# Moving the weight sums and differences of seven-product matmuls from VectorE to GpSimd, and shifting a prefetch by one step

## The chip, the cores and the metric

The kernel runs on one core of a Trainium2 chip. The metric is the device time of one execution in microseconds; three executions of the kernel before gave 2406.97, 2407.13 and 2408.5 us, so the median is 2407.13 us and the runs lie within 0.06% of each other.

## The reference

The program is a small diffusion backbone in float32 with two layers, 512 latent tokens and 256 context tokens, width 1024. Layer 0 is SwiGLU, short gated convolution, SwiGLU; layer 1 is SwiGLU, grouped-query attention, SwiGLU. Each of the six sub-layers normalizes, scales and shifts its input by vectors that come from a conditioning vector ("modulation"), and its output is added through a third such vector, the gate.

```
def swiglu(h, w_in, w_out):
    gate, up = jnp.split(h @ w_in, 2, axis=-1)
    return (jax.nn.silu(gate) * up) @ w_out

m_lat = (silu_c @ ada_w[i] + ada_b[i]).reshape(b, N_SUBLAYERS, N_MOD, 1, d)
h = norm_modulate(x_lat, norm_g[i, 0], m_lat[:, 0, 0], m_lat[:, 0, 1])
x_lat = x_lat + MACARON_WEIGHT * m_lat[:, 0, 2] * swiglu(h, ffn_w_in[i, 0], ffn_w_out[i, 0])
```

The first matmul of the SwiGLUs (1024 to 2 x 2816) and of the convolution (1024 to 3 x 1024) carries most of the arithmetic. The modulation weights `ada_w` are 1024 x 9216 for each layer.

## The kernel before, in words

**Stages.** The stages are named f00, c01, f02 (layer 0), f10, attention and f12 (layer 1); f12 handles only the 512 latent tokens, the others all 768. Activations lie with the width on the partitions and the tokens along the free axis, weights are the stationary operand. Every float32 operand is split into a high part and a low rest (`split`, line 188: the high part by ScalarE, line 189, the rest by VectorE, line 190), and every product is three matmuls (`mm3`, lines 861 to 863: high x high, high x low, low x high).

**The seven products.** The input matmul of f00, c01, f02, f10 and f12 is done by a Strassen scheme. For each column chunk c, two weight columns blocks (a gate block g and an up block u, 1024 x 128 each) are cut into two halves along the contraction: quarters 0 and 1 of g, 2 and 3 of u, each 128 x 512 in SBUF. Seven products M1 to M7, each of four contraction steps of three matmuls over half the tokens (384, in f12 256), replace eight. M1, M2, M4 and M7 need quarters or quarter results as they stand; M5, M6 and M3 need sums or differences. These are made in place in the raw weight tile (`add_product`, lines 368 to 397): for M5, quarter 0 becomes 0 minus 2 (line 373) and quarter 2 becomes 2 plus 3 (line 382); for M6, quarter 2 becomes 3 minus 0 (line 373 again, called at 385); for M3, quarter 1 becomes 1 minus 2. So each chunk takes four such operations of 128 x 512, three by line 373 and one by line 382. There are 88 chunks. In the first chunks of each stage the products are plain ("direct"), without sums. `product_order` (line 89) gives the order on TensorE; in the steady state it is M1(c), M2(c), M7(c-1), M5(c), M6(c), M4(c-1), M3(c-1). After groups of four chunks the output matmul of the SwiGLU comes in between ("out").

**Weights on their way.** Raw weights come from HBM by DMAs that SyncE issues (line 230) into five buffers `raw` (two more in f12). The split results go into a store of eight buffers ("granules", tag `w`, line 256). `w_fill` (line 268) makes granules in the order in which TensorE will use them, as far ahead as the store has room; at the beginning of f12 only three ahead (`AHEAD`). One granule serves one product.

**Evictions.** ScalarE and VectorE also empty PSUM: M1, M5 and M6 are copied by ScalarE (lines 1135, 1140, 1143), M2, M7, M3 and M4 are added to those copies by VectorE (lines 1137, 1146, 1151, 1204), the output matmuls by line 929 on VectorE.

**Modulation in the background.** From f00 on, modulation vectors of the later sub-layers are computed on VectorE beside the products: `ada_step` (line 522) multiplies a 128 x 512 tile `aw` of modulation weights with the conditioning vector and sums along the row (line 530, an instruction and a short accumulator read for each of up to two conditioning vectors). `bg` spreads these steps evenly over the products and output matmuls of a stage. The tiles come by DMAs which GpSimd issues (`ada_next`, line 504, DMA at line 509); they rotate through 4 buffers in f00, 2 in c01 and 5 in f02 and f10. At the end of step n the kernel asks for tile n + depth, into the buffer which step n has just read.

**Order.** TensorE and SyncE run in the written order throughout; VectorE and ScalarE do so in the opening of each stage. Elsewhere, and on GpSimd always, a scheduler fixes each engine's order when the program is built, by the written order and its own costs. At run time each engine works through its queue in that order, and an instruction that waits for a semaphore holds up all behind it on its engine.

Of the kernel before, what the change touches and what calls it, by code (L numbers as in the profile page):

```python
# [14 lines left out]
ALU = mybir.AluOpType  # L15
# [114 lines left out]
def backbone(ctx: ExitStack, tc: tile.TileContext, a: dict, out: bass.AP):  # L130
    nc = tc.nc
    act, dve, pe = nc.scalar, nc.vector, nc.tensor
# [21 lines left out]
    def ptile(name, shape=(P, 512)):  # L154
        pool, tag = bank[name]
        return pool.tile(list(shape), F32, name=f"ps_{name}", tag=tag)
# [31 lines left out]
    def split(dsth, dstl, src, pinned=False):  # L188
        hi = act.activation(dsth, src, AF.Copy)  # L189
        lo = dve.tensor_tensor(out=dstl, in0=src, in1=dsth.bitcast(F32), op=ALU.subtract)  # L190
        if pinned:
            tc.keep_in_program_order(hi)
            tc.keep_in_program_order(lo)
# [44 lines left out]
    def raw_used(n):  # L238
        raw_tiles[n][1] -= 1
        if not raw_tiles[n][1]:  # L240
            raw_tiles.pop(n)
            if n in raw_extra["held"]:
                raw_extra["open"] -= 1
            elif n not in raw_homes:
                raw_state["open"] -= 1
# [122 lines left out]
    def add_product(g, u, m):  # L368
        def quad(q):
            return raw_tiles[g if q < 2 else u][0][:, 0, slice(4 * (q % 2), 4 * (q % 2) + 4)]  # L370

        def sub(o, x, y):
            dve.tensor_tensor(out=quad(o), in0=quad(x), in1=quad(y), op=ALU.subtract)  # L373

        def make(dh, dl):
            if m == "M1":
                split(dh, dl, quad(0))
            elif m == "M2":
                split(dh, dl, quad(1))
            elif m == "M5":  # L380
                sub(0, 0, 2)
                dve.tensor_tensor(out=quad(2), in0=quad(2), in1=quad(3), op=ALU.add)
                split(dh, dl, quad(2))
            elif m == "M6":
                sub(2, 3, 0)
                split(dh, dl, quad(2))
            elif m == "M7":
                split(dh, dl, quad(0))
            elif m == "M4":
                split(dh, dl, quad(3))  # L390
            else:
                sub(1, 1, 2)
                split(dh, dl, quad(1))
                raw_used(g)
                raw_used(u)

        stream.append((None, None, 4, make))
# [103 lines left out]
    ada_chunks, ada_loaded, ahead = [], {}, {}  # L501
    silu_row = {}

    def ada_next(n):

        if n < ahead["limit"]:
            t, kh, j = ada_chunks[n]
            w = ada_loaded[n] = ahead["pool"].tile([P, 512], F32, name=f"aw{t}_{kh}_{j}", tag="aw", bufs=ahead["depth"])
            nc.gpsimd.dma_start(w, a["ada_t"][t, kh, j])  # L509
# [12 lines left out]
    def ada_step(n, i, hm, nv):  # L522

        t, kh, j = ada_chunks[n]
        w = ada_loaded.pop(n)
        col = 4 * (hm % 2) + j
        for v in range(nv):
            total = mods[i][:, hm // 2, col, v : v + 1]
            junk = ptile("S")
            ins = dve.tensor_tensor_reduce(out=junk, in0=w, in1=silu_row[kh][:, v, :], scale=1.0, scalar=total if kh else ada_b[:, i, hm // 2, col : col + 1], op0=ALU.mult, op1=ALU.add, accum_out=total)  # L530
            tc.keep_in_program_order(ins)
        ada_next(n + ahead["depth"])
        if kh and j == 3:
            ada_done.add((i, hm))

    def ada_list():


        tasks = [(i, hm) for i in range(2) for hm in range(18) if i or hm > 5]
        at = 0  # L540
        for key, end in ADA_BY.items():
            steps = []
            for kh in range(2):
                steps += [lambda kh=kh: silu_load(kh)] + [rest] * 3
                for t in range(at, end):
                    i, hm = tasks[t]
                    for j in range(4):
                        steps.append(lambda n=len(ada_chunks), i=i, hm=hm: ada_step(n, i, hm, mod_groups(i, hm // 2)))
                        ada_chunks.append((t, kh, j))
            ada_tasks.extend((at, go) for go in steps)  # L550
            at = end
# [1149 lines left out]
    with tc.tile_pool(name="apool", bufs=1) as apool, tc.tile_pool(name="g0", bufs=1) as gp, tc.tile_pool(name="qp", bufs=1) as qp, psum(A=3, B=1, C=3, S=1):  # L1701
# [24 lines left out]
        with tc.tile_pool(name="boot", bufs=1) as bp, aw_pool():  # L1726
            in_order()
            op = opening(0, 0)
# [166 lines left out]
```

## Time and profile before

| what | value |
|---|---|
| median of three runs | 2407.13 us |
| span of the profiled execution | 2405.2 us |
| TensorE busy (matmuls) | 2383.8 us, 99% |
| VectorE busy | 2033.0 us, 85% |
| ScalarE busy | 1164.8 us, 48% |
| GpSimd busy | 135.2 us, 6% |
| sums and differences on VectorE | 352 instructions, 181.5 + 60.4 us |
| loads of modulation tiles issued by GpSimd | 240, 129.1 us |

The span runs from the first to the last instruction of the profiled execution; the runs' times lie about 2 us above it. A row of the groups gives line, engine, operation, output and inputs, shape and count, then busy time and mean ns, then the idle time of that engine just before such instructions and what ended it. A row of the waits gives the total in us, how often, and the longest. A row of the windows gives, for a stretch in us from the start, each engine's busy time with its number of instructions, then the granted TensorE clock, the DMA share and GB/s. In the timeline a row is start, duration, engine, line, operation.

### The profile page before, as it was taken

The numbers are of one execution on the slowest core, as the hardware profiler recorded it, in microseconds if no ns is written. First come the engines' busy times: TensorE is split into PE (matmuls) and PEld (weight loads), VectorE is DVE, ScalarE is ACT, GpSimd is POOL, SyncE is SP. The second block draws the span as 40 slices with busy tenths as digits, with TensorE's granted clock in tenths as the row PEclk, the third lists the DMA queues.
The fourth block names the chain that finished last, engine by engine and source line by source line (L and its number), as shares of the span: only waits on it lengthen the run. The fifth ranks groups of instructions, "written<-read, shape, count | busy, mean of one in ns | idle before, by whom it ended". The sixth has DMA issues, their size and how long they took to land.

```text
span 2405.2 us, 37639 instructions
## 1 busy us (share of the span) xinstructions
PE 2383.8 (99%) x14303; PEld 2258.6 (94%) x14303; DVE 2033.0 (85%) x4018; ACT 1164.8 (48%) x2198; POOL 135.2 (6%) x256
## 2 busy tenths in 40 slices
PE   8999999999999999999999999999999999999998
PEld 6999999999999999999999999999998889999998
DVE  6989989978988888888887988888778987987787
ACT  5634334355535653433435543343355776555555
POOL 0001111100000001000000001101100000000000
PEclk9999999999999999999999999999999999999999
DMA  9234444430334123323432144443441101133331
GB/s 334 87 112 137 130 126 129 131 115 27 106 106 132 33 69 115 127 93 119 126 100 73 49 124 126 146 136 122 141 131 45 53 10 58 67 110 102 106 106 62
DMA packets 93062, 253.71 MB, mean 105 GB/s; under 512 B 10320, under 2 KB 18640, under 8 KB 92880
## 3 DMA queue, kind: packets, MB, share of 16 engines
q1 hardware_dynamic: 71984, 183.65, 23.5%
q0 software_dynamic: 20352, 67.12, 9.4%
q8 instruction: 112, 1.84, 0.3%
q14 instruction: 70, 0.57, 0.1%
q10 hardware_dynamic: 544, 0.52, 0.1%
HBM read 249.16 MB, written 2.10 MB: 104 GB/s over the span
## 4 chain that ended last, share of the span: by engine, by line
PE 92%; DVE 3%; ACT 2%; DMA 1%; issue 1%; SPq 0%; DVEq 0%; ACTq 0%
PE ps_A L861 16%; PE ps_A L862 16%; PE ps_A L863 16%; PE ps_C L862 11%; PE ps_C L861 11%; PE ps_C L863 11%; PE ps_B L863 3%; PE ps_B L861 3%; PE ps_B L862 3%; PE ps_T L1542 1%; DMA ada<-in_ada_w 1%; ACT pr L1525 0%; DMA raw<-in_ffn_w_in 0%; DVE w L190 0%; PE ps_O L861 0%
## 5 line engine op out<-in xcount | busy, mean ns | idle before, releaser
L189 ACT ACTIVATE w<-raw 128x512 fp32r<-128x512 f32 (+1 forms) x862 | 522.4, 619 | 721.0 <-PE ps_A L863 229.7
L190 DVE TENSOR_TENSOR w<-raw,w 128x512 fp32r<-128x512 f32 (+1 forms) x862 | 574.3, 679 | 119.7 <-ACT w L189 105.8
L509 POOL DMA_DIRECT2D aw<-in_ada_t x240 | 129.1, 538 | 1374.8 <-DVE mods L530 973.9
L373 DVE TENSOR_TENSOR raw<-raw,raw 128x512 f32<-128x512 f32 x264 | 181.5, 689 | 9.0 <-DMA raw<-in_ffn_w_in 4.9
L862 PE MATMUL ps_C<-gl,w 128*128 128x512 f32 (+1 forms) x548 | 188.5, 344 | 0.0
L861 PE MATMUL ps_C<-gh,w 128*128 128x512 f32 (+1 forms) x548 | 188.4, 344 | 0.0
L863 PE MATMUL ps_C<-gh,w 128*128 128x512 f32 (+1 forms) x548 | 188.2, 343 | 0.0
L861 PE MATMUL ps_A<-gh,w 128*128 128x512 f32 (+1 forms) x540 | 185.8, 344 | 0.6 <-DVE x L929 0.6
L862 PE MATMUL ps_A<-gl,w 128*128 128x512 f32 (+1 forms) x540 | 185.7, 344 | 0.0
L863 PE MATMUL ps_A<-gh,w 128*128 128x512 f32 (+1 forms) x540 | 185.5, 344 | 0.0
L530 DVE CUSTOM_DVE_ANT_0 ps_S<-aw,silu_row,packed 128x512 f32<-128x512 f32 x208 | 156.9, 754 | 2.4 <-DMA aw<-in_ada_t 1.0
L530 DVE CUSTOM_DVE_ANT_0 ps_S<-aw,silu_row,mods 128x512 f32<-128x512 f32 x208 | 156.8, 754 | 1.0
L929 DVE SCALAR_TENSOR_TENSOR x<-ps_C,gat,x 128x512 f32<-128x512 f32 (+1 forms) x158 | 99.5, 631 | 43.1 <-PE ps_C L863 42.7
L861 PE MATMUL ps_A<-tB11h,w 128*128 128x384 f32 (+1 forms) x400 | 130.8, 327 | 0.2 <-ACT tB11h L785 0.2
L862 PE MATMUL ps_A<-tB11l,w 128*128 128x384 f32 (+1 forms) x400 | 130.3, 326 | 0.2 <-DVE tB11l L786 0.2
L863 PE MATMUL ps_A<-tB11h,w 128*128 128x384 f32 (+1 forms) x400 | 130.4, 326 | 0.0
L862 PE MATMUL ps_C<-tB22l,w 128*128 128x384 f32 (+2 forms) x376 | 121.8, 324 | 0.0
L863 PE MATMUL ps_C<-tB22h,w 128*128 128x384 f32 (+2 forms) x376 | 121.7, 324 | 0.0
L861 PE MATMUL ps_C<-tB22h,w 128*128 128x384 f32 (+2 forms) x376 | 121.5, 323 | 0.0
L929 DVE SCALAR_TENSOR_TENSOR x<-ps_A,gat,x 128x512 f32<-128x512 f32 (+1 forms) x162 | 101.8, 637 | 17.0 <-PE ps_A L863 16.7
L863 PEld LDWEIGHTS ps_C<-gh,w 128*128 128x128 f32 x548 | 103.9, 190 | 12.3
L861 PEld LDWEIGHTS ps_A<-gh,w 128*128 128x128 f32 x540 | 102.4, 190 | 14.0 <-issue 1.0
(486 smaller groups left out, 6946.0 us busy)
## 6 DMA issues: line engine op xcount, KB each, us to landing
raw<-in_ffn_w_in SPq DMA_DIRECT2D x170, 512.0 KB, 3.7
aw<-in_ada_t POOLq DMA_DIRECT2D x240, 256.0 KB, 3.0
raw<-in_ffn_w_out SPq DMA_DIRECT2D x80, 512.0 KB, 4.1
raw<-in_conv_w_in SPq DMA_DIRECT2D x24, 512.0 KB, 3.7
ada<-in_ada_w SPq DMA_DIRECT2D x28, 256.0 KB, 5.7
raw<-in_attn_w_qkv SPq DMA_DIRECT2D x12, 512.0 KB, 4.9
raw<-in_ada_w SPq DMA_DIRECT2D x8, 512.0 KB, 6.8
silu_row<-in_crow POOLq DMA_DIRECT2D x8, 512.0 KB, 4.2
```

The source lines that it names most:

```text
L189: hi = act.activation(dsth, src, AF.Copy)
L190: lo = dve.tensor_tensor(out=dstl, in0=src, in1=dsth.bitcast(F32), op=ALU.subtract)
L373: dve.tensor_tensor(out=quad(o), in0=quad(x), in1=quad(y), op=ALU.subtract)
L509: nc.gpsimd.dma_start(w, a["ada_t"][t, kh, j])
L530: ins = dve.tensor_tensor_reduce(out=junk, in0=w, in1=silu_row[kh][:, v, :], scale=1.0, scalar=total if kh else ada_b[:, i, hm // 2, col : ...
L861: pe.matmul(ps, wh, xh, start=first, stop=False, **kw)
L862: pe.matmul(ps, wh, xl, start=False, stop=False, **kw)
L863: pe.matmul(ps, wl, xh, start=False, stop=last, **kw)
L929: dve.scalar_tensor_tensor(out=x, in0=p[:, o - off : o - off + w], scalar=gat[:, m, v : v + 1], in1=x, op0=ALU.mult, op1=ALU.add)
L1542: pe.transpose(pt[:, c, :], pr[:, (c0 + c) * P : (c0 + c + 1) * P], ident)
```

## The change

`sub` and the sum for M5 are issued on GpSimd instead of VectorE, with the same operands. `ada_step` n no longer asks for tile n + depth but for tile n - 1 + depth, into the buffer that step n - 1 has read; the first step of each stage asks for nothing. The 240 loads remain, each one step later.

```diff
         def sub(o, x, y):
-            dve.tensor_tensor(out=quad(o), in0=quad(x), in1=quad(y), op=ALU.subtract)
+            nc.gpsimd.tensor_tensor(out=quad(o), in0=quad(x), in1=quad(y), op=ALU.subtract)
...
             elif m == "M5":
                 sub(0, 0, 2)
-                dve.tensor_tensor(out=quad(2), in0=quad(2), in1=quad(3), op=ALU.add)
+                nc.gpsimd.tensor_tensor(out=quad(2), in0=quad(2), in1=quad(3), op=ALU.add)
                 split(dh, dl, quad(2))
...
             tc.keep_in_program_order(ins)
-        ada_next(n + ahead["depth"])
+        if n > ahead["start"]:
+            ada_next(n - 1 + ahead["depth"])
```

## The prediction

> **What bounds the kernel now.** I read the page first, then TensorE's waits, then the stages in windows.
>
> ```profile
> span 2405.2 us, 37639 instructions
> PE 2383.8 (99%) x14303; PEld 2258.6 (94%) x14303; DVE 2033.0 (85%) x4018; ACT 1164.8 (48%) x2198; POOL 135.2 (6%) x256
> DVE  6989989978988888888887988888778987987787
> ```
>
> TensorE is idle for 2405.2 - 2383.8 = 21.4 us in all. VectorE is the next engine, with slices at 90% or more. A busy TensorE need not be one at its own pace, so the pace has to be shown. The windows show it:
>
> ```profile
> 120.00:480.00 360.00, 360.00 (x2068) 344.85 (x2067) 328.61 (x697) 138.78 (x254) 41.41 (x77) 1.00 0.42 128
> 600.00:780.00 180.00, 180.00 (x1032) 176.21 (x1032) 161.95 (x360) 84.52 (x161) 10.76 (x20) 1.00 0.37 115
> 900.00:1260.00 360.00, 360.00 (x2067) 344.85 (x2066) 301.69 (x599) 136.82 (x251) 30.65 (x57) 1.00 0.37 113
> 1380.00:1740.00 360.00, 360.00 (x2067) 344.85 (x2066) 302.88 (x599) 138.73 (x254) 45.17 (x84) 1.00 0.43 132
> 2040.00:2100.00 60.00, 57.74 (x426) 54.13 (x426) 57.54 (x112) 35.87 (x76) 0.00 (x0) 1.00 0.17 59
> 2100.00:2340.00 240.00, 240.00 (x1680) 224.99 (x1679) 194.73 (x350) 125.15 (x253) 0.00 (x0) 1.00 0.33 108
> ```
>
> Columns after the length: PE, PEld, DVE, ACT, POOL. The three long SwiGLU stretches (f00 at 120, f02 at 900, f10 at 1380) put 2068, 2067 and 2067 matmuls through in 360 us, though VectorE is 91%, 84% and 84% busy in them. So TensorE's pace there doesn't depend on how full VectorE is. That is the heart of the forecast: relief for VectorE has nothing to buy in these stretches. Of these rows only 2040 to 2100, the opening of f12, has TensorE idle (60 - 57.74 = 2.3 us), with VectorE 96% full.
>
> Why VectorE's lateness doesn't reach TensorE is seen from ScalarE's waits and the timeline:
>
> ```profile
> ACT w L189 <- PE ps_A L863: 229.7, 154, 9.0
> ACT w L189 <- PE ps_C L863: 213.9, 111, 11.9
> ACT w L189 <- PE ps_B L863: 56.7, 69, 1.2
> ```
> ```profile
> 700.43 0.34 PE L861 MATMUL ps_B<-tB21h,w 128*128 128x384 f32 x1
> ...
> 702.28 0.68 DVE L382 TENSOR_TENSOR raw<-raw 128x512 f32<-128x512 f32 x1
> ...
> 702.54 0.34 PE L861 MATMUL ps_A<-tT3h,w 128*128 128x384 f32 x1
> ...
> 702.88 0.55 DVE L1137 TENSOR_TENSOR g<-ps_B,g 128x384 f32<-128x384 f32 x1
> ```
>
> In 154 + 111 + 69 = 334 of 862 splits ScalarE stood waiting for TensorE to give a granule back, which means that the store was full. M2 began at 700.43 and the next product at 702.54: a product takes 2.11 us, and seven granules ahead are 14.8 us of cover.
>
> **The change, part by part.**
>
> *Removed from VectorE.*
>
> ```profile
> L373 DVE TENSOR_TENSOR raw<-raw,raw 128x512 f32<-128x512 f32 x264 | 181.5, 689 | 9.0 <-DMA raw<-in_ffn_w_in 4.9 <-DMA raw<-in_conv_w_in 0.2
> L382 DVE TENSOR_TENSOR raw<-raw 128x512 f32<-128x512 f32 x88 | 60.4, 687 | 0.7
> L190 DVE TENSOR_TENSOR w<-raw,w 128x512 fp32r<-128x512 f32 (+1 forms) x862 | 574.3, 679 | 119.7 <-ACT w L189 105.8
> L189 ACT ACTIVATE w<-raw 128x512 fp32r<-128x512 f32 (+1 forms) x862 | 522.4, 619 | 721.0 <-PE ps_A L863 229.7 <-PE ps_C L863 213.9 <-DVE raw L373 68.1
> ```
>
> There are 264 + 88 = 352 instructions. The timeline's line 382 began at 702.28 and the next instruction at 702.88, so one takes 0.60 us of VectorE's queue: 352 x 0.60 = 211 us. On TensorE's path it is worth nothing in the five long stretches (idle 0) and at most the 2.3 us in f12's opening, plus the one wait of 0.6 us for line 929 in the last row of TensorE's waits below: a best case of about 3 us.
>
> *Added to GpSimd.* The trace has no GpSimd operation with two inputs. The nearest rows:
>
> ```profile
> L1884 POOL MEMSET const-float32-1.0<- 128x1 f32 x1 | 0.1, 98 | 0.0
> masks.py:197 POOL MEMSET ident<- 128x128 f32 x1 | 0.2, 204 | 103.4 <-DVE tl L637 103.4
> masks.py:199 POOL TENSOR_SCALAR_AFFINE_SELECT identb<-identb 128x128 f32<-128x128 f32 x1 | 0.3, 292 | 0.1
> masks.py:199 POOL TENSOR_SCALAR_AFFINE_SELECT ident<-ident 128x128 f32<-128x128 f32 x1 | 0.8, 772 | 0.1
> ```
>
> A write alone costs (204 - 98) / 127 = 0.83 ns per element, one read and a write (292 - 98) / 127 = 1.53 ns. A second read at the same difference of 0.70 ns makes 2.23 ns, or 0.10 + 512 x 2.23 ns = 1.24 us. The bounds are 0.88 us (the second read free) and 1.66 us (it doubles the instruction less its start). I take 1.24, since the added read is nearest to the read already seen. That is 352 x 1.24 = 436 us of new GpSimd work, 18% of the span: GpSimd is not the bound.
>
> [...]
>
> *Latency of the sums.* For M5 two operations take 2.5 us instead of 1.3, for M6 one takes 0.6 us more. The quarters that M5 overwrites are free once M1 is split, three granules earlier, so 6.3 us are there for 2.5. M6's difference waits for M5's split: 0.62 + 0.68 + 1.24 = 2.5 us against one product's 2.1, 0.4 us late, covered by the 14.8. Behind a ScalarE split that waits stand ScalarE's evictions (lines 1135, 1140, 1143); the tightest, M6's, must be done before M7, two products or 4.2 us later. Price: 0. In f12's opening the store is only three ahead and the cover is gone. TensorE's waits there:
>
> ```profile
> PE ps_C L861 <- ACT w L189: 0.7, 1, 0.7
> PE ps_C L863 <- DVE w L190: 0.5, 1, 0.5
> PE ps_A L861 <- DVE x L929: 0.6, 1, 0.6
> ```
>
> The first two rows lie there: the first f12 product with a sum (M5, bank C) was waited for already. Its two operations add 1.2 us if exposed, less what VectorE's relief gives back: bounds -2.3 and +1.8 (M6's 0.6 too), I take +1.0 us.
>
> *What a busy GpSimd does to VectorE.* Two rows show that they get in each other's way:
>
> ```profile
> 1836.75 0.69 DVE L190 TENSOR_TENSOR w<-raw,w 128x512 fp32r<-128x512 f32 x1 [0.33 <-ACT w L189]
> ```
> ```profile
> 1836.82 0.77 POOL masks.py:199 TENSOR_SCALAR_AFFINE_SELECT ident<-ident 128x128 f32<-128x128 f32 x1
> ```
>
> The same select that took 0.29 us beside an idle VectorE took 0.77 us when VectorE had begun a two-input operation 0.07 us earlier, and ended 0.15 us after it. GpSimd waited; the opposite order isn't in the trace. So one GpSimd operation costs VectorE between 0 (GpSimd always yields) and 1.24 us (VectorE stands for all of it). I take half, 0.62: part of VectorE's work, like line 1137, reads one operand from PSUM, and with VectorE 84 to 91% full GpSimd will mostly be the one that waits. Then VectorE loses 0.62 for each 0.60 that it saves: its load stays as it was, and so does its cover. With f00 as the fullest stretch: 49 + 16 = 65 operations (rows below), 328.6 - 39.0 + 40.3 = 330 of 360 us. Price: 0.
>
> *Loads one step later.*
>
> ```profile
> L509 POOL DMA_DIRECT2D aw<-in_ada_t x240 | 129.1, 538 | 1374.8 <-DVE mods L530 973.9 <-DVE c L1146 178.4 <-DVE g L1137 49.2
> aw<-in_ada_t POOLq DMA_DIRECT2D x240, 256.0 KB, 3.0
> ```
>
> GpSimd now waits for VectorE's step before nearly each load. With sums behind it in the queue, such a wait would hold the sums; asked one step later, the buffer is mostly free already. SP's queue is not passed. The lead shrinks to depth - 1 steps: three or four steps in the SwiGLUs, one in c01, where a load must issue (0.54) and land (3.0) within one step.
>
> ```profile
> 600.00:780.00 180.00, 26.06 (x64) 1.00 0.37 115
> ```
>
> That is line 530 alone in c01: 64 records, four to a step, 16 steps in 180 us, 11 us apart on average. 3.5 us, or 6.0 behind two sums, fits. Price: 0.
>
> **Sum:** 2405.2 + 0 (long stretches) + 1.0 (f12's opening) = 2406.2 us of span; the median lies 2407.13 - 2405.2 = 1.9 us above the profiled span: 2408.1 us.
>
> **The rivals.**
>
> *Slower: the shared way into SBUF fills VectorE.* Line 373 by stage (VectorE's part), a third of it to be added for line 382:
>
> ```profile
> 120.00:480.00 360.00, 33.25 (x49) 1.00 0.42 128
> 600.00:780.00 180.00, 16.57 (x24) 1.00 0.37 115
> 900.00:1260.00 360.00, 31.02 (x45) 1.00 0.37 113
> 1380.00:1740.00 360.00, 33.10 (x48) 1.00 0.43 132
> 2100.00:2340.00 240.00, 33.04 (x48) 1.00 0.33 108
> ```
>
> So 65, 32, 60, 64 and 64 operations. If each stops VectorE for its full 1.24 us, f00 needs 328.6 - 39.0 + 80.6 = 370.2 of 360 us and c01 161.95 - 19.2 + 39.7 = 182.4 of 180; the others (340, 344, 236 of 240) just fit. TensorE then follows VectorE: +10.2 + 2.4 = 12.6, about 2420 us. It decides from (360 - 328.6 + 39.0) / 65 = 1.08 us of VectorE per operation. At 1.66 us the five stretches would run over by 37.5, 15.9, 5.3, 10.7 and 22.5, together 92 us: 2499. For it speaks that all these operands lie in SBUF and the 0.77 us row; against it that most collisions should fall on GpSimd. Chance 0.27.
>
> [...]
>
> *Slower: late through GpSimd's queue.* Sums stand behind a load that still waits, or c01's tiles come late. If each of c01's 16 steps stood 3.5 us for its tile, VectorE would be at 162 + 56 = 218 of 180 us: +38, 2445. The distance of 11 us speaks against it. Chance 0.08.
>
> *Faster by over 0.2%.* 0.2% is 4.8 us, about what a measurement of this kernel can tell from no change. The idle time in reach is the 3 us above; to get 2402 the f12 opening would have to lose all its waits and the start (where a few sums lie among the first 120 us) some too. Chance 0.07.
>
> **How the numbers follow.** My forecast, within 0.2%: 0.58. Faster 0.07; slower 0.27 + 0.08 = 0.35. Its own range is 2405 to 2411. The range for all reaches from 2402, nearly the whole gain in reach, to 2440, which takes in the exclusion up to about 1.4 us per operation and leaves out its worse end and most of the late loads.
>
> **What would show it.** Right: the five stretches again hold 2068, 1032, 2067, 2067 and 1680 matmuls with TensorE idle 0; lines 373 and 382 stand under POOL at 1.1 to 1.4 us; VectorE's busy time is 1.9 to 2.1 ms, with its two-input rows longer. Wrong: matmuls of lines 861 to 863 wait for line 190 or 189 in f00 (exclusion), or line 530 waits for `aw` in c01 (late loads), or GpSimd rows of 2 us and more.

## The result and the profile after

The changed kernel takes 2451.34 us (median of 4 runs, 2450.06 to 2452.7), the kernel before 2407.05 us beside it. The ratio is 1.0185, 95% interval 1.0173 to 1.0197: slower by about 44 us. The forecast was 2408.1 us, in a range that ended at 2440.

The page of the changed kernel:

```profile
span 2448.3 us, 37886 instructions
PE 2395.6 (98%) x14303; PEld 2264.0 (92%) x14303; DVE 1997.3 (82%) x3666; ACT 1156.2 (47%) x2198; POOL 639.5 (26%) x608
```

VectorE has 352 instructions fewer, and its busy time fell, from 2033.0 to 1997.3 us. GpSimd is busy for a quarter of the span. Nevertheless TensorE's idle time rose from 21.4 to 2448.3 - 2395.6 = 52.7 us. So a total of busy time doesn't tell what happened; the windows tell where. These are the stretches of the prediction, columns PE, PEld, VectorE, ScalarE, GpSimd:

```profile
120.00:480.00 360.00, 351.69 (x2006) 335.66 (x2005) 316.19 (x613) 130.74 (x243) 130.52 (x137) 1.00 0.41 125
600.00:780.00 180.00, 171.51 (x962) 165.03 (x961) 155.61 (x299) 75.35 (x147) 60.54 (x51) 0.99 0.30 92
900.00:1260.00 360.00, 360.00 (x2067) 344.82 (x2066) 296.14 (x536) 138.00 (x251) 116.40 (x114) 1.00 0.35 109
1380.00:1740.00 360.00, 359.45 (x2056) 345.20 (x2056) 292.79 (x527) 145.68 (x266) 134.85 (x142) 1.00 0.42 129
2040.00:2100.00 60.00, 59.33 (x471) 57.27 (x470) 50.96 (x107) 37.65 (x76) 1.58 (x1) 1.00 0.19 63
2100.00:2340.00 240.00, 229.85 (x1598) 214.35 (x1597) 179.21 (x283) 117.40 (x251) 88.18 (x65) 0.99 0.30 99
```

Count matmuls: f00 has 2006 where there were 2068, c01 962 where there were 1032, f12 1598 where there were 1680. At 360/2068 = 0.174 us a matmul (f12: 240/1680 = 0.143) that is 10.8, 12.2 and 11.7 us. f02 lost none. f10 has 2056, but it was busy for 359.45 us of its window, which by now holds other products than before, since everything there begins some 28 us later. The two stretches that lost nothing or little, f02 and f10, have nearly as many GpSimd operations as f00 (60 and 64 against 65). Matching each matmul of one trace with the same one of the other gives the same picture: +10.9 us in f00, +12.4 in c01, +13.5 in f12, at most 0.4 in f02 and f10, the rest in the pieces between. Of the 43.3 us in all, 35.6 come in 24 single jumps of over 0.3 us (in the time from the start of one matmul to the next; two more at 7 and 11 us wait for a DMA). TensorE kept its pace and then stood still for a moment, 24 times.

The jumps come at fixed places. By the clock of the kernel before, those in f00's stretch lie at 186.5, 278.5, 370.5 and 462.5 us, one for each group of four chunks, at the first product behind the output matmuls. In f12 four lie 61.5 us apart, at the same place of each group, where M4 begins.

What TensorE stood for, from its waits (total, times, longest):

```profile
PE ps_A L862 <- DVE x L930: 12.2, 7, 2.5
PE ps_A L862 <- DVE c L1147: 11.7, 7, 2.6
PE ps_B L864 <- DVE w L190: 4.0, 3, 1.6
PE ps_A L862 <- ACT g L1136: 2.9, 2, 1.7
```

Lines behind 532 are one higher than before. The longest waits are not for a weight granule (line 190) but for evictions: a product wants bank A, and VectorE hasn't emptied it yet (line 930 after an output matmul; line 1147 after M7, whose result must be read before M4 adds to it).

And these are the groups that pay. The operations moved to GpSimd, the splits, the loads, one eviction, and line 373 by itself (shortest/median/longest):

```profile
L190 DVE TENSOR_TENSOR w<-raw,w 128x512 fp32r<-128x512 f32 (+1 forms) x862 | 701.1, 827 | 224.8 <-ACT w L189 215.2 <-PE ps_B L864 0.3
L373 POOL TENSOR_TENSOR raw<-raw,raw 128x512 f32<-128x512 f32 x264 | 367.9, 1394 | 868.1 <-DVE w L190 720.5
L382 POOL TENSOR_TENSOR raw<-raw 128x512 f32<-128x512 f32 x88 | 136.2, 1548 | 6.8
L509 POOL DMA_DIRECT2D aw<-in_ada_t x240 | 131.0, 546 | 589.9 <-DVE mods L530 417.6
L930 DVE SCALAR_TENSOR_TENSOR x<-ps_C,gat,x 128x512 f32<-128x512 f32 (+1 forms) x158 | 98.8, 628 | 42.9 <-PE ps_C L864 42.8
```
```profile
L373 POOL TENSOR_TENSOR raw<-raw,raw x264: 1263/1297/1925, 75.0 to 2398.5; 128x512 f32<-128x512 f32 x132
```

The split (line 190), which reads two tiles in SBUF, went from 679 to 827 ns. Line 930, which reads one operand from PSUM, stayed at 628 (631 before). Next come line 530's multiplications, which also read two tiles in SBUF, with 813 ns instead of 754. Nothing else of the program's work became longer to this extent.

The trace also shows it one by one. 178 splits of 128x512 began while a sum ran on GpSimd, and 175 of them ended between 0.54 and 0.56 us after that sum did, whenever they had begun. The 66 instructions of line 930 that ran beside a sum took as long as the others (740 ns against 746 at 128x512, 474 against 477 at 128x256).

One of the jumps, in f12, from the timeline:

```profile
2138.30 0.41 DVE L1138 TENSOR_TENSOR g<-ps_B,g 128x256 f32<-128x256 f32 x1
2138.51 1.26 POOL L373 TENSOR_TENSOR raw<-raw,raw 128x512 f32<-128x512 f32 x1 [3.16 <-DVE w L190]
2138.63 1.69 DVE L190 TENSOR_TENSOR w<-raw,w 128x512 fp32r<-128x512 f32 x1
...
2139.85 1.59 POOL L382 TENSOR_TENSOR raw<-raw 128x512 f32<-128x512 f32 x1
2140.24 0.41 DVE L1147 TENSOR_TENSOR c<-ps_A,c 128x256 f32<-128x256 f32 x1
...
2140.71 0.58 PE L862 MATMUL ps_A<-tT4h,w 128*128 128x256 f32 x1 [2.25 <-DVE c L1147]
```

GpSimd began its difference at 2138.51. VectorE began a split 0.12 us later, stood until GpSimd had ended at 2139.77, did its work in 0.55 us and was done at 2140.32: 1.69 us instead of 0.68. Behind the split in VectorE's queue was the eviction of bank A, and M4 waited for it. TensorE had been idle for 2.25 us, some 1.0 of them by this stop (1.69 - 0.68); the rest is lateness that the queue already had. GpSimd's next operation, begun at 2139.85 while VectorE was still at work, took 1.59 us where 1.26 to 1.30 are the rule: here a split held up GpSimd, by some 0.3 us.

### The profile page after: what moved, and what is told of

Read it like the earlier page. It is cut to its first block, busy times and chain, and to the rows that moved or that the text cites. A ratio compares the mean times of both kernels' runs of the same rounds, so it can differ in the third digit from the quotient of the medians.

```text
span 2448.3 us, 37886 instructions
## 1 busy us (share of the span) xinstructions
PE 2395.6 (98%) x14303; PEld 2264.0 (92%) x14303; DVE 1997.3 (82%) x3666; ACT 1156.2 (47%) x2198; POOL 639.5 (26%) x608
## 4 chain that ended last, share of the span: by engine, by line
PE 70%; DVE 14%; issue 9%; ACT 3%; DMA 2%; POOL 1%; SPq 0%; DVEq 0%; ACTq 0%; POOLq 0%
PE ps_A L862 13%; PE ps_A L863 13%; PE ps_A L864 12%; PE ps_C L862 8%; PE ps_C L863 8%; PE ps_C L864 8%; DVE w L190 4%; DVE ps_S L530 4%; PE ps_B L864 2%; PE ps_B L862 2%; PE ps_B L863 2%; DVE x L930 1%; POOL raw L373 1%; DMA ada<-in_ada_w 1%; ACT w L189 1%
## 5 line engine op out<-in xcount | busy, mean ns | idle before, releaser
L190 DVE TENSOR_TENSOR w<-raw,w 128x512 fp32r<-128x512 f32 (+1 forms) x862 | 701.1, 827 | 224.8 <-ACT w L189 215.2
L373 POOL TENSOR_TENSOR raw<-raw,raw 128x512 f32<-128x512 f32 x264 | 367.9, 1394 | 868.1 <-DVE w L190 720.5
L530 DVE CUSTOM_DVE_ANT_0 ps_S<-aw,silu_row,packed 128x512 f32<-128x512 f32 x208 | 170.1, 818 | 3.4 <-DMA aw<-in_ada_t 1.2
L530 DVE CUSTOM_DVE_ANT_0 ps_S<-aw,silu_row,mods 128x512 f32<-128x512 f32 x208 | 167.9, 807 | 1.9
L382 POOL TENSOR_TENSOR raw<-raw 128x512 f32<-128x512 f32 x88 | 136.2, 1548 | 6.8
L862 PE MATMUL ps_A<-tT4h,w 128*128 128x384 f32 (+1 forms) x352 | 117.4, 333 | 11.7 <-DVE c L1147 11.7
L189 ACT ACTIVATE gh<-g 128x384 fp32r<-128x384 f32 (+1 forms) x158 | 78.7, 498 | 90.9 <-DVE g L1205 46.1
```

Source lines behind the costliest of these rows:

```text
L373: nc.gpsimd.tensor_tensor(out=quad(o), in0=quad(x), in1=quad(y), op=ALU.subtract)
L382: nc.gpsimd.tensor_tensor(out=quad(2), in0=quad(2), in1=quad(3), op=ALU.add)
L862: pe.matmul(ps, wh, xh, start=first, stop=False, **kw)
```

## The experiments

The theory: a GpSimd operation that reads SBUF and a VectorE instruction with two SBUF inputs exclude each other, VectorE's queue stops for the rest of the GpSimd operation, and the evictions behind the stopped instruction come late for TensorE. The rivals: the loads that come a step later; the sums that come later, since they take GpSimd longer and cross two engines; another order of VectorE's queue, since the scheduler plans with other costs.

**The two parts of the change apart.** `loads_only` keeps the sums on VectorE; `sums_only` keeps the loads as before.

```diff
 loads_only, against the changed kernel
-            nc.gpsimd.tensor_tensor(out=quad(o), in0=quad(x), in1=quad(y), op=ALU.subtract)
+            dve.tensor_tensor(out=quad(o), in0=quad(x), in1=quad(y), op=ALU.subtract)
...
-                nc.gpsimd.tensor_tensor(out=quad(2), in0=quad(2), in1=quad(3), op=ALU.add)
+                dve.tensor_tensor(out=quad(2), in0=quad(2), in1=quad(3), op=ALU.add)
 sums_only, against the changed kernel
-        if n > ahead["start"]:
-            ada_next(n - 1 + ahead["depth"])
+        ada_next(n + ahead["depth"])
```

Expected of `loads_only`: 

> Only the loads one step later; the sums stay on VectorE. If the sums cost the time: 2406 to 2409 us, no change. If the later loads cost it (tiles of c01 come late): 2420 us or more, with line 530 waiting for aw in c01.

Expected of `sums_only`: 

> The sums and differences go to GpSimd, the loads of modulation tiles stay as they were (asked for at the end of step n for tile n + depth). If the sums cost the time, by exclusion from SBUF, by lateness or by the order in which the scheduler then puts VectorE's queue: 2440 to 2460 us, near the changed kernel's 2451. If the loads one step later cost it: 2407 us. If the shift of the loads protects the sums from waiting behind a load on GpSimd: slower than 2451, by up to some 20 us.

Measured: `loads_only` 2406.78 us, ratio 1.0001 [0.9992, 1.001]; `sums_only` 2448.45 us, ratio 1.0176 [1.0161, 1.0191]. The loads cost nothing; the sums carry all of it, within the 3 us between `sums_only` and the changed kernel.

**Late sums without reads.** In `write_only` the sums are left out on all engines. In their place, in the same tiles and with the same waits, GpSimd writes a constant three times. VectorE and ScalarE run the same instructions as in `sums_only`. Their order was expected to be the same too, but by the traces it isn't: some 80 of VectorE's 3666 instructions and some 65 of ScalarE's 2198 stand elsewhere. At 122 us, for instance, an eviction (line 1204 of `sums_only`) comes ahead of two splits instead of behind them.

```diff
-            nc.gpsimd.tensor_tensor(out=quad(o), in0=quad(x), in1=quad(y), op=ALU.subtract)
+            for _ in range(3):
+                nc.gpsimd.memset(quad(o), 0.5)
...
-                nc.gpsimd.tensor_tensor(out=quad(2), in0=quad(2), in1=quad(3), op=ALU.add)
+                for _ in range(3):
+                    nc.gpsimd.memset(quad(2), 0.5)
```

Expected: 

> Leaves out the sums: GpSimd writes a constant into the same quarter three times instead, with the same waits for it, so that it is about as long busy (an estimated 3 x 0.53 = 1.6 us from the memset rows) but reads nothing from SBUF. The scheduler gives VectorE and ScalarE exactly the order of sums_only. Exclusion theory: VectorE's two-input instructions are back at 0.68 us and the time at 2405 to 2415 us. Lateness theory (splits and what stands behind them wait for GpSimd): 2440 to 2460 us as with real sums. Order theory: also 2440 to 2460 us.

Measured: 2403.47 us, ratio 0.9987 [0.9978, 0.9997]. Its groups and a row of its waits:

```profile
L374 POOL MEMSET raw<- 128x512 f32 x792 | 410.6, 526 | 310.7 <-DVE w L190 286.6
L190 DVE TENSOR_TENSOR w<-raw,w 128x512 fp32r<-128x512 f32 (+1 forms) x862 | 574.4, 679 | 285.8 <-ACT w L189 274.0
```
```profile
ACT w L189 <- POOL raw L374: 126.1, 83, 4.8
```

Three writes take 3 x 0.526 = 1.58 us, longer than a sum did. ScalarE waits 126.1 us for GpSimd, VectorE in turn 274.0 us for ScalarE, and TensorE loses nothing: the store covers late sums, as the prediction had it. The split is back at 679 ns. What is missing here is GpSimd's reading. The run is not the whole proof, for two reasons: its order differs, and ScalarE waits longer in the changed kernel (173.1 + 60.5 = 233.6 us). The next pair has neither weakness.

**Reads without late sums.** `no_sums` leaves the sums out on all engines. `lock_only` leaves them out too, but GpSimd makes 352 operations with two SBUF inputs at their places, whose results no split reads (the splits of M7 and M3 take another quarter for that). VectorE's and ScalarE's instructions are the same in both, and by the traces so is their order, except for four of VectorE's instructions in c01.

```diff
 no_sums, against the changed kernel
-            nc.gpsimd.tensor_tensor(out=quad(o), in0=quad(x), in1=quad(y), op=ALU.subtract)
+            pass
...
-                nc.gpsimd.tensor_tensor(out=quad(2), in0=quad(2), in1=quad(3), op=ALU.add)
 lock_only, against the changed kernel
-                sub(0, 0, 2)
-                nc.gpsimd.tensor_tensor(out=quad(2), in0=quad(2), in1=quad(3), op=ALU.add)
+                beside(0, quad(0), quad(2))
+                beside(0, quad(2), quad(3))
...
-                sub(2, 3, 0)
+                beside(0, quad(3), lows[-1].bitcast(F32))
...
-                sub(1, 1, 2)
-                split(dh, dl, quad(1))
+                beside(1, quad(1), quad(2))
+                split(dh, dl, quad(2))
```

Here `beside` is a subtraction on GpSimd with the given operands, and `lows[-1]` is the low granule of the split just made.

Expected of `no_sums`: 

> Leaves out the sums altogether, on all engines; the splits read the quarters as they were loaded. VectorE's order differs from the changed kernel's in few places. Exclusion and lateness theories: 2403 to 2408 us, which is also the most that taking the sums off VectorE could ever bring. Order theory (evictions planned behind other work): 2430 us or more.

Expected of `lock_only`: 

> Leaves out the sums as no_sums does, with the same order on VectorE and ScalarE; beside the splits GpSimd does two-input operations of the same size, place and number (352), whose result no split reads, so that nothing on the way of a weight waits for GpSimd. No_sums was 2402.15 us. If exclusion from SBUF alone makes the loss: 2430 to 2455 us, with line 190 near 0.82 us. If it takes exclusion together with splits that wait for GpSimd: 2402 to 2412 us though line 190 is slow.

Measured: `no_sums` 2402.15 us, ratio 0.9982 [0.9973, 0.9992]; `lock_only` 2444.81 us, ratio 1.0158 [1.0141, 1.0175]. The difference of 42.7 us is made by operations that no compute engine waits for. (SyncE's loads of raw weights do wait for them, 77 times, but the weights don't come late: ScalarE waits 13.4 us for feed-forward weights in `lock_only`, 16.8 in `no_sums`.) Matched with `no_sums`, `lock_only` loses 11.0 us in f00, 9.9 in c01, 11.1 in f12 and at most 0.1 in f02 and f10: the same stages as the changed kernel, with nearly the same amounts.

`no_sums` also speaks against another order of the queues as the cause. Between it and the changed kernel some 40 of VectorE's instructions and 16 of ScalarE's stand elsewhere, only 2 of them in f00 and 6 in f12, and `no_sums` loses nothing in either stage.

From the pages, the groups and the windows (f00) of `no_sums`:

```profile
PE 2382.1 (99%) x14303; PEld 2258.5 (94%) x14303; DVE 1839.2 (77%) x3666; ACT 1167.9 (49%) x2198; POOL 135.1 (6%) x256
```
```profile
L190 DVE TENSOR_TENSOR w<-raw,w 128x512 fp32r<-128x512 f32 (+1 forms) x862 | 577.4, 679 | 251.5 <-ACT w L189 233.8
```
```profile
120.00:480.00 360.00, 360.00 (x2068) 344.81 (x2067) 296.27 (x630) 137.45 (x252) 41.41 (x77) 1.00 0.42 128
```

and of `lock_only`, with its windows for f00 and f02 and TensorE's first two waits:

```profile
PE 2395.3 (98%) x14303; PEld 2263.7 (93%) x14303; DVE 2068.3 (85%) x3666; ACT 1163.4 (48%) x2198; POOL 668.5 (27%) x608
```
```profile
L190 DVE TENSOR_TENSOR w<-raw,w 128x512 fp32r<-128x512 f32 (+1 forms) x862 | 740.3, 872 | 132.3 <-ACT w L189 123.3
```
```profile
120.00:480.00 360.00, 352.32 (x2005) 335.63 (x2004) 328.16 (x612) 130.84 (x241) 131.56 (x137) 1.00 0.41 125
...
900.00:1260.00 360.00, 360.00 (x2067) 344.81 (x2066) 307.35 (x532) 136.19 (x250) 119.34 (x115) 1.00 0.35 107
```
```profile
PE ps_A L863 <- DVE c L1148: 11.0, 9, 3.9
PE ps_A L863 <- DVE x L931: 9.2, 8, 2.2
```

VectorE does the same work in both, so the difference of its busy times is time in which it stood: 2068.3 - 1839.2 = 229 us, 0.65 us for each of 352 operations. In the changed kernel it is 1997.3 - 1839.2 = 158 us, 0.45 us each. TensorE waits for the same two evictions. The f00 row against that of the kernel before is the most instructive pair: VectorE is busy for 328.16 us here and for 328.61 us before, and here TensorE loses 63 matmuls, before none. Equal load, unequal loss.

**One input instead of two.** `lock_one_input` is `lock_only` with each operation replaced by two copies, each of which reads one tile (the sums stay left out).

```diff
-            nc.gpsimd.tensor_tensor(out=quad(o), in0=x, in1=y, op=ALU.subtract)
+            for t in (x, y):
+                nc.gpsimd.tensor_copy(quad(o), t)
```

Expected: 

> As lock_only, but each two-input operation is replaced by two copies with one input each (sums left out). If any GpSimd operation that reads SBUF stops VectorE's two-input instructions: line 190 above 0.75 us and 2425 us or more. If GpSimd needs two inputs for that: line 190 at 0.68 us and 2402 to 2405 us.

Measured: 2416.05 us, ratio 1.0039 [1.0024, 1.0054].

```profile
L376 POOL COPY raw<-raw 128x512 f32<-128x512 f32 x616 | 521.0, 864 | 684.4 <-DVE w L190 636.7 <-DVE bias L1230 24.9 <-ACT w L189 3.2
L190 DVE TENSOR_TENSOR w<-raw,w 128x512 fp32r<-128x512 f32 (+1 forms) x862 | 637.4, 749 | 197.1 <-ACT w L189 182.9
```

(The other 88 of the 704 copies read a granule and stand in a row of their own.) One read is enough to stop VectorE (749 ns against 679), though 704 copies cost only 13.9 us over `no_sums`. That lies between the two times that were expected: the stops came, but only a third of `lock_only`'s loss. Why is not shown.

**How the loss goes with the number of operations.** Three kernels make fewer of the sums on GpSimd: `f02_f10_only` those of f02 and f10, 160; `m5_on_vector` those for M6 and M3, 176; `m5_sum_on_vector` the three differences, 264.

```diff
 f02_f10_only: sub and the sum for M5 take an engine eng
+                add_product(raw[c, 0], raw[c, 1], m, nc.gpsimd if key in ("f02", "f10") else dve)
 m5_on_vector
+            (dve if m == "M5" else nc.gpsimd).tensor_tensor(out=quad(o), in0=quad(x), in1=quad(y), op=ALU.subtract)
 m5_on_vector and m5_sum_on_vector
-                nc.gpsimd.tensor_tensor(out=quad(2), in0=quad(2), in1=quad(3), op=ALU.add)
+                dve.tensor_tensor(out=quad(2), in0=quad(2), in1=quad(3), op=ALU.add)
```

Expected of `f02_f10_only`: 

> Sums on GpSimd in f02 and f10 alone, on VectorE in f00, c01 and f12. In the changed kernel's trace the stretches of f02 and f10 lost 0.0 and 0.4 us and their openings 1.8 each, so if each stage stands for itself: 2406 to 2411 us. If the loss moves with the order or with the total: 2420 us or more.

Expected of `m5_on_vector`: 

> Only the single differences of M6 and M3 (176) go to GpSimd; M5's pair stays on VectorE. If the loss goes with the number of stops: about half of the 44 us, 2422 to 2432 us. If it comes from the two back-to-back operations of M5, which keep VectorE out for up to 2.7 us at once: 2405 to 2413 us.

Expected of `m5_sum_on_vector`: 

> All three differences on GpSimd (264 operations), only M5's sum (line 382) on VectorE, so that no two GpSimd operations follow each other directly. The changed kernel with 352 lost 44 us, m5_on_vector with 176 lost 7. If the back-to-back pair makes the loss: 2410 to 2420 us. If the loss goes with the number or the total of the stops: 2430 us or more.

Measured: 2410.74 us, ratio 1.0017 [1.0008, 1.0026]; 2413.39 us, ratio 1.0027 [1.0016, 1.0037]; 2438.07 us, ratio 1.0128 [1.0112, 1.0143]. In `f02_f10_only` the long stretches lose 0.4 us between them; the loss lies in the openings of the two stages. So the first came out as expected for stages that stand for themselves. The second lies just above the range that it was given if M5's pair makes the loss, and the third in the range for the number or the total of the stops; the two don't agree on one of these causes. (The pairs of M5 took 2.65 us or more in the changed kernel, but its longest split took 2.08: none was seen to be kept out for a whole pair.) The third isn't a clean test, since its VectorE makes the sum for M5 and waits for GpSimd's difference first:

```profile
DVE raw L382 <- POOL raw L373: 92.0, 59, 3.1
```

So I took the clean kernels, `lock_only` cut in two. `lock_pair` keeps only the two operations at M5, one right behind the other, `lock_single` only those at M6 and M3; 176 each, the sums left out as in `no_sums`.

```diff
 lock_pair, against lock_only
-                beside(0, quad(3), lows[-1].bitcast(F32))
...
-                beside(1, quad(1), quad(2))
 lock_single, against lock_only
-                beside(0, quad(0), quad(2))
-                beside(0, quad(2), quad(3))
```

Expected of `lock_pair`: 

> Left out: all sums and differences of weight quarters, as in no_sums. GpSimd makes 176 operations with two SBUF inputs that nothing reads, at the places of M5's two, one right behind the other; the 176 of M6 and M3 are not made. VectorE and ScalarE run the same instructions in the same order as in no_sums (2402.2 us) and lock_only (2444.8 us). If the loss goes with the number of stops, half of lock_only's 42.6 us: 2421 to 2426 us, as in lock_single. If it is the back to back pair that makes VectorE late, most of it: 2435 us or more. If the loss grows faster than the number, as the sums on GpSimd suggest (176 of them cost 7 us, 264 cost 31, 352 cost 44): under 2415 us.

Expected of `lock_single`: 

> Left out: all sums and differences of weight quarters, as in no_sums. GpSimd makes 176 operations with two SBUF inputs that nothing reads, at the places of M6's and M3's differences, each alone; the pair of M5 is not made. VectorE and ScalarE as in no_sums. If the loss goes with the number of stops: 2421 to 2426 us, the same as lock_pair. If the pair of M5 makes it: 2403 to 2412 us. If the loss grows faster than the number: under 2415 us here and in lock_pair too.

Measured: 2411.64 us, ratio 1.0019 [1.001, 1.0029], and 2408.21 us, ratio 1.0005 [0.9996, 1.0014]. The page and f00 of `lock_pair`, then of `lock_single`:

```profile
PE 2383.8 (99%) x14303; PEld 2258.2 (94%) x14303; DVE 1951.0 (81%) x3666; ACT 1165.5 (48%) x2198; POOL 402.5 (17%) x432
```
```profile
120.00:480.00 360.00, 357.67 (x2052) 342.12 (x2051) 316.70 (x628) 135.48 (x248) 89.26 (x107) 1.00 0.41 125
```
```profile
PE 2383.9 (99%) x14303; PEld 2258.6 (94%) x14303; DVE 1925.7 (80%) x3666; ACT 1166.8 (48%) x2198; POOL 386.4 (16%) x432
```
```profile
120.00:480.00 360.00, 358.59 (x2055) 342.82 (x2054) 314.06 (x627) 135.98 (x249) 85.03 (x107) 1.00 0.42 126
```

Over `no_sums` the pairs cost 9.5 us, the single ones 6.1, together 15.6; all of them in one kernel cost 42.7. Both are under 2415 us, as was expected if the loss grows faster than the number. VectorE stood for (1951.0 - 1839.2) / 176 = 0.64 us and (1925.7 - 1839.2) / 176 = 0.49 us per operation, against 0.65 in `lock_only`. So the loss is neither a price per stop nor the work of the pair alone. It looks as if the first stops met a reserve, and the next ones reached TensorE once it was used up; the runs show the growth, not the reserve itself.

**Attempts to mend it.** `halves` cuts each GpSimd operation of the changed kernel into two of 128 x 256, so that a stop ends sooner. `f12_m4_later` puts M3 ahead of M4 in f12, which gives the late eviction behind M7 one product more; `f12_m4_later_vector` is the same order in the kernel before, as a control.

```diff
 halves
+            for z in (slice(0, 2), slice(2, 4)):
+                nc.gpsimd.tensor_tensor(out=quad(o)[:, z], in0=quad(x)[:, z], in1=quad(y)[:, z], op=ALU.subtract)
 f12_m4_later, f12_m4_later_vector
-        order += [(c, "M1"), (c, "M2"), (c - 1, "M7"), (c, "M5"), (c, "M6"), (c - 1, "M4")]
+        order += [(c, "M1"), (c, "M2"), (c - 1, "M7"), (c, "M5"), (c, "M6"), (c - 1, "M3" if m4_last else "M4")]
```

Expected of `halves`: 

> The changed kernel with each GpSimd operation cut into two of 128 x 256: twice as many, each about half as long, the same operands in all. The order on VectorE stays nearly the same. If VectorE gets in between two GpSimd operations, its longest stop is halved: 2415 to 2435 us. If GpSimd keeps VectorE out through successive operations, or the total of the stops decides: 2445 to 2460 us.

Expected of `f12_m4_later`: 

> The changed kernel, but in f12 M3 of a chunk comes before its M4, so that three products instead of two lie between M7 and M4, which has to wait until VectorE has read M7's result out of the same bank. The stops of VectorE stay. If late reads of M7 make f12's loss of 13.5 us (2100 to 2340): it falls to 0 to 5 us, in all 2438 to 2445 us. If VectorE's total load makes it: 2449 to 2453 us.

Expected of `f12_m4_later_vector`: 

> The same order of f12's products in the kernel before, sums on VectorE: the control. TensorE is never late there, so 2405 to 2409 us.

Measured: `halves` 2451.51 us, ratio 1.0187 [1.0172, 1.0202]; `f12_m4_later` 2449.9 us, ratio 1.0179 [1.0164, 1.0194]; the control 2408.88 us, ratio 1.0009 [1.0, 1.0019]. The first row is of `halves`, the others are TensorE's waits in `f12_m4_later`:

```profile
L374 POOL TENSOR_TENSOR raw<-raw,raw 128x256 f32<-128x256 f32 x528 | 434.1, 850 | 814.5 <-DVE w L190 664.5
```
```profile
PE ps_A L865 <- ACT g L1139: 7.5, 9, 2.8
PE ps_A L865 <- DVE c L1150: 4.0, 4, 2.6
```

Two halves take 2 x 0.850 = 1.70 us where the whole took 1.39; nothing is won. With M4 later the wait for M7's eviction shrinks from 11.7 to 4.0 us, and the next eviction, ScalarE's copy of M1, takes its place with 7.5 instead of 2.9. In f12 alone (2100 to 2360 us) the first falls from 7.8 to 0.5 us and the second rises from 1.2 to 5.9. Moving one deadline is no cure here. All three times lie in ranges that were given beforehand: `halves` in the one for the total of the stops (or a GpSimd that holds on through successive operations), `f12_m4_later` in the one for VectorE's total load, the control in its own. No version that makes the sums beats the kernel before. `no_sums`, which does without the sums altogether, is only 4.4 us faster in its own comparison: that is about all that any relief of VectorE could have won.

## Why the prediction was wrong

**What bounds the kernel, and the relief for VectorE: right.** 211 us off VectorE were priced at no more than 3 us. Without any sums, `no_sums` gains 4.4 us (0.18%); matched by matmul, 2.9 us of it lie in f12's opening, where the prediction had seen 2.3.

**The added GpSimd operation: right.** 1.24 us was taken; alone it takes 1.26 to 1.30 us. GpSimd, at 639.5 us or 26% of the span, never became the bound.

**Latency of the sums: right.** The price of 0 is what `write_only` measured, with slower writes than sums, though in another order of the queues. The +1.0 us for f12's opening is lost in the rest: the matched matmuls give +0.3.

**Loads one step later: right.** Price 0, measured by `loads_only`.

**What a busy GpSimd does to VectorE: the step that failed.** Its size came out near: 0.62 us per operation was taken, 0.45 us (changed kernel) and 0.65 us (`lock_only`) were measured. That was luck, since 0.62 was the middle between two bounds, and the reason given for it was wrong: "GpSimd will mostly be the one that waits". GpSimd's excess over its 1.30 us is 264 x 0.094 + 88 x 0.248 = 47 us, VectorE's is 158. But what made the error of 43 us is the last line of the step, "330 of 360 us. Price: 0". It took a stretch as one sum: as long as VectorE's work fits in, TensorE loses nothing. The forecast had seen that TensorE's pace did not depend on how full VectorE was in the kernel before, and took that for a rule. VectorE's load in f00 came out even lower than the 330 us, at 316, and TensorE lost 10.9 us there. `lock_only` has that load in f00, 328 us, and loses 11 us there. A removed sum is 0.60 us of planned work; a stop comes where a split meets an operation on GpSimd (175 of 178 times in the changed kernel), lengthens a split by up to 1.4 us (the longest took 2.08), and may stand right ahead of an eviction. The cover of 14.8 us that was named holds for weight granules. M7's eviction has two products, 4.2 us in f00 and (24 matmuls of 0.117 us each) 2.8 us in f12. The eviction of an output matmul that held f00 up has two shorter output matmuls in which to be done, 275.55 to 278.42 us in `no_sums`, or 2.9 us. The 4.2 us stood in the prediction for ScalarE's evictions; VectorE's were not held against any such number. So the sign that the forecast named for exclusion, matmuls in f00 that wait for line 190 or 189, did not show: TensorE's waits in that stretch are all for line 930.

**The rival "slower by exclusion": right that VectorE is made to stand, wrong in its price.** It used the same sum of a stretch, so that it was to decide from 1.08 us per operation. It decided at 0.45, and the largest loss (by matched matmuls) came in f12, where the rival had 236 of 240 us and VectorE was in fact at 179. What the runs show of such stops: a split that began beside a sum on GpSimd ended 0.54 to 0.56 us after it in 175 of 178 cases (the longest split took 2.08 us); a sum that began beside a split took 1.59 us instead of 1.26 to 1.30; one-input copies on GpSimd lengthen the splits too (749 ns), writes alone do not (679); and line 930, which reads one of its two large operands from PSUM, stayed at 628 (631 before). That a shared way into SBUF is what lies behind it, as the rival's name has it, is not shown.

**What stays open.** Why f00, c01 and f12 lose and f02 and f10 do not. f00 with 88% of VectorE busy and f12 with 75% lie on both sides of f02 at 82%, so load alone doesn't order them. That f12's products are a third shorter fits it for f12. The cover of 2.9 us behind the output matmuls doesn't set f00 apart: f02 has the same (1129.92 to 1132.79 us in `no_sums`). The modulation steps might: in `no_sums` they fill 128.5 us of VectorE in f00's stretch, 91.1 in f02's and 88.6 in f10's. No run tests this. Nor is it settled why the changed kernel, with 158 us of stops, loses as much as `lock_only` with 229. ScalarE waits for late sums in the changed kernel, 49.9 us in f00 and 51.2 in f12 against 23.9 and 20.1 in `write_only`, and not at all in `lock_only`; that these waits and the stops add up is argued, not shown. TensorE's busy time rose by 2395.6 - 2383.8 = 11.8 us; some 4.6 us of that are the slow clock below, the rest was not resolved.

## What to carry to other kernels

Before work is moved to GpSimd, list which of VectorE's frequent instructions read two operands from SBUF, and count a stop for each meeting (here 0.45 to 0.65 us of VectorE per GpSimd operation). Don't add these stops to a stretch's busy time: look at what stands behind the stopped instruction in its queue, and hold one stop, then two or three in a row, against the tightest deadline there. A deep store of weights (14.8 us of cover here) doesn't cover PSUM evictions that share its engine (here 2.8 to 4.2 us).

## What the runs showed of the hardware that was not expected

Some of TensorE's idle moments cost more than their length. The granted clock in the first long stop, f00 of the changed kernel (columns after TensorE and loads as above; the clock is the last but two):

```profile
191.00:195.00 4.00, 4.00 (x15) 4.00 (x15) 2.96 (x8) 0.70 (x2) 1.49 (x2) 0.57 0.51 121
```

After an idle time of 2.50 us the clock fell, to 0.57 in the mean of this row and 0.50 between 191.6 and 195.0; matmuls began 0.32 us apart instead of 0.175 until 3.41 us had passed. That happened three times in the changed kernel (at 191.6, 761.6 and 2140.6 us) and cost about 1.5 us each time (in f00 10.7 matmuls, each 0.145 us later), some 4.6 us of the 43. The idle times ahead of them were 2.50, 2.65 and 2.25 us; two others, of 2.49 us (until 381.0) and 2.32 us (until 103.7), had no such drop.

One difference between the two kinds can be read from this trace. The three slow stretches lasted 3.413 us each, and they began 570.03 and 1378.98 us apart, 167.0 and 404.0 times that length. If that is a grid that runs through the whole trace, the three idle times ahead of a drop fell, but for 0.1 us of the last, into one step of it (2.50, 2.65 and 2.16 us), and the two without a drop lay across an edge, with at most 1.72 and 1.44 us in one step. The grid is an estimate from these three drops. What lowers the clock, and from which idle time on, is not shown.
